# Up-projection as seven block products instead of eight, with weight-block sums made ahead

## The chip, the cores and the metric

One core of a Trainium2 chip runs the whole kernel. Its engines are TensorE (PE for the matrix products and PEld for their weight loads in the profile), VectorE (DVE), ScalarE (ACT), GpSimd (POOL) and SyncE (SP, which here only issues DMAs). The metric is the device time of one execution in microseconds (us), the median of several runs.

## The reference, cut to what matters

A decoder layer runs over 2048 prompt tokens and 64 sample tokens (8 sequences of 8). The first part (projections, sliding-window attention, the RWKV-7 recurrence) is not touched in what it computes. The second part is, per token:

```python
x = x + (g_a * (att @ w_pa) + g_b * (rw_out @ w_pb)) @ w_o
h = rmsnorm(x, norm2_g)
ug, uv = jnp.split(h @ w_up, 2, axis=-1)        # w_up: 1024 x 5632
c = conv_b + sum(conv_w[j] * ucat[:, j:j + T] for j in range(3))   # ucat: ug with 2 earlier rows
x = x + (jax.nn.gelu(c) * uv) @ w_down          # w_down: 2816 x 1024
y = rmsnorm(x, final_g)
```

## The kernel before, in words

The kernel has two phases. Phase 1 (`phase1`, `group1`) goes through the tokens in six groups, makes the combined input projection, attention and recurrence, and stores their outputs and the gates in DRAM (`outs_d`, `gates_d`). Its order on TensorE is written out: `mm` ties each product to the one before (`ordered`), and side work (attention, recurrence, the bias tables) runs as generators that yield a number of nanoseconds and are resumed when the planned time `now` has moved on by that much (`spawn`, `poll`, `drain`). The weights of the input projection come through the SP queue (`load_w`).

Phase 2 (`phase2`, `group2`) takes three groups of T = 704 tokens. All data is transposed: features on partitions, tokens along the free dimension. A product of fp32 quality is made of three products of rounded halves: both operands are split into a rounded part `hi` and a rest `lo`, and hi·hi, hi·lo and lo·hi are summed in PSUM. Weights are split as they arrive: `load_w` fetches up to [128, 8, 128] numbers, `split_w` lets ACT copy them into `whi` (L383) and `wsub` (L424) subtracts to get `wlo`; every second `wsub` goes to GpSimd (`pool_every` 2), the others to VectorE. Raw weights and their two halves share one pool tag of seven slots (`W_SLOTS`, `wtile`). Activations are split by ACT and VectorE in `split` (L1319 to L1323).

Each token group is two chunks of 352 columns; `gemm` (L471) goes over the k tiles, per k tile over the three passes, and per pass over both chunks, so a loaded weight tile serves two products of 352 columns. In a group come, in this order:

- eight output tiles of `w_ab` (attention and recurrence halves), gated on VectorE, added on GpSimd (L1386), split into `mix`;
- eight output tiles of `w_o`, added to x (L1399); VectorE and ACT split x times the norm weight into `h2` (L1323), and sum the squares (L1333);
- 22 pairs of feed-forward tiles in parts of 4, 6, 6 and 6: `up(f)` makes the `w_ug` tile, multiplies it by the row norm `rs` while taking it out of PSUM (L1427), runs the convolution (L1431, L1437) and the GELU (L1445 to L1448), and GpSimd multiplies by `rs` once more (L1449); `gate(f, s)` makes the `w_uv` tile, multiplies (L1456) and splits (L1323). The norm itself (`rstd_steps`) thus has the length of the first `up` product to finish in;
- after each part, eight output tiles of `w_down` over the 4 or 6 tiles of the part, added to x (L1478).

The final norm of a group (`final`) is spawned beside the next group's `w_ab`; for the last group it is the tail, made per chunk so that the first chunk's norm falls among the second chunk's last products.

Of the kernel before, what the change touches and what calls it, by code (L numbers as in the profile page):

```python
# [9 lines left out]
F32 = mybir.dt.float32  # L10
F32R = mybir.dt.float32r
# [68 lines left out]
Y_rwkv_post_2 = 1205  # L80
W_AT = (1, 5)
# [90 lines left out]
class Build:  # L172
# [315 lines left out]
    def phase1(self):  # L488
        nc, tc, cfg, A = self.nc, self.tc, self.cfg, self.A
        with ExitStack() as ctx:  # L490
# [4 lines left out]
                             at=AT_SLOTS, PTm=4, carry=2, sp=3, nrm=3, gm=2, gsq=1, XV=XV_SLOTS, Z=3, sm=8)  # L495
            self.pbufs = dict(acc=2, psA=2, ps=3, psY=1)
            self.cp1 = cp1
            self.rw = cfg.tmax + 9
            self.prev = dict(carry=None, vt=None, S=None)
# [91 lines left out]
    def group1(self, g, t0, n, samp, last):  # L591
# [72 lines left out]
        if g == 0:  # L664
            self.spawn(self.bias_tables())
        G.ready = 0
# [628 lines left out]
    def phase2(self):  # L1295
        nc, tc, cfg, A = self.nc, self.tc, self.cfg, self.A
        with ExitStack() as ctx:
# [3 lines left out]
            self.bufs = dict(A=16, B=16, x2=8, th=4, tm=2, ub=2, cc=2, ss=2, ssq=1, carry=2, nrm=3)  # L1301
            self.pbufs = dict(acc=8)
            for tag in ("B", "x2"):
                self.t(tag, [128, cfg.tmax2])
# [9 lines left out]
    def split(self, src, tag, T, scale=None):  # L1314
# [3 lines left out]
        if scale is None:  # L1318
            nc.scalar.copy(out=hi[:, :T], in_=src[:, :T])  # L1319
            nc.vector.tensor_tensor(out=lo[:, :T], in0=src[:, :T], in1=hi[:, :T].bitcast(F32), op=SUB)  # L1320
        else:
            nc.scalar.mul(out=hi[:, :T], in_=src[:, :T], mul=scale)  # L1322
            nc.vector.scalar_tensor_tensor(out=lo[:, :T], in0=src[:, :T], scalar=scale, in1=hi[:, :T].bitcast(F32), op0=MUL, op1=SUB)  # L1323
        return hi, lo

    def sumsq(self, ssq, x, m, T):
        nc = self.nc
        if m == 0:
            nc.scalar.activation(out=ssq[:, :T], in_=x[:, :T], func=AF.Square)
        else:  # L1330
            sq = self.t("ss", [128, self.cfg.tmax2])
            nc.scalar.activation(out=sq[:, :T], in_=x[:, :T], func=AF.Square)
            nc.vector.tensor_tensor(out=ssq[:, :T], in0=ssq[:, :T], in1=sq[:, :T], op=ADD)  # L1333

    def load_outs(self, c0, c1):
        self.outs, T = [], c1 - c0
        for k in range(8):
            o = self.t("th", [128, self.cfg.tmax2])
            self.last_load = self.nc.gpsimd.dma_start(out=o[:, :T], in_=self.outs_d[k][:, c0:c1]).ins.name
            self.outs.append(self.split(o, "A", T))  # L1340
# [18 lines left out]
    def group2(self, g, c0, c1):  # L1359
# [8 lines left out]
        chunks = [(i * w, (i + 1) * w if i < nchk - 1 else T) for i in range(nchk)]  # L1368
        if g == 0:
            self.load_outs(c0, c1)  # L1370
        outs = self.outs
        mix = []
        if g:
            done = self.spawn(self.later(L_SSQ, self.final(*self.done)))
        for m in range(8):
            hi, lo = self.weights("w_ab", m)
            self.nopool = False
            pa = self.gemm(hi, lo, outs[:4], 0, chunks, "acc")
            pb = self.gemm(hi, lo, outs[4:], 0, chunks, "acc", wk0=4)
# [7 lines left out]
            mix.append(self.split(ta, "B", T, 0.5))  # L1387

        if g:
            self.drain(done)  # L1390
        x2, h2 = [], []
        rs = self.t("ssq", [128, TM])
        for m in range(8):
            hi, lo = self.weights("w_o", m)
            ps = self.gemm(hi, lo, mix, 0, chunks, "acc")
            x = self.t("x2", [128, TM])
            nc.gpsimd.dma_start(out=x[:, :T], in_=A["x"][m][:, c0:c1])
            for (a, b), pp in zip(chunks, ps):
                nc.vector.tensor_tensor(out=x[:, a:b], in0=x[:, a:b], in1=pp[:, :b - a], op=ADD)  # L1399
            h2.append(self.split(x, "A", T, self.v("n2", m)))  # L1400
            self.sumsq(rs, x, m, T)
            x2.append(x)
        norm = self.spawn(self.later(L_SSQ, self.rstd_steps(rs, T, "acc")))
# [5 lines left out]
        while f < cfg.ff:  # L1409
            e = f + (cfg.ff - f - 1) % 6 + 1  # L1410
            parts.append(list(range(f, e)))
# [199 lines left out]
```

## Time and profile before

| | us |
|---|---|
| median of 3 runs (lowest, highest) | 3439.56 (3434.27, 3441.33) |
| profiled execution, run time | 3443.16 |
| profiled execution, span of the trace | 3441.4 |
| mean granted TensorE clock in it | 0.974 of 2.4 GHz |

Busy time of an engine is the union of its instructions' spans. The spans of products overlap their neighbours' (a 352-column product shows 0.32 us and the next one starts 0.16 us later), so a price per product is taken from the count of products in a stretch without idle time. The same holds, by some 0.08 us, for VectorE instructions that follow each other at once.

### The profile page before, as it was taken

To read this page: it belongs to the slowest core of one execution; us is meant where nothing else is said; L and a number is where in the kernel's file an instruction comes from. 1 tells how busy PE (TensorE), PEld (TensorE's weight loads), DVE (VectorE), ACT (ScalarE), POOL (GpSimd) and SP (SyncE) were. 2 spreads that over 40 slices of the span, in tenths; PEclk is the share of its full clock that TensorE was granted. 3 is DMA by queue.
4 is the path that set the end of the run, shared out by engine and by line. 5 is a ranking of instruction groups with operands and counts; after the bars stand their busy time and mean duration, and the time that the engine had idled before them with its cause. 6 is when DMAs were issued, how large, how long until landed. Compare 5 with 4: busy or idle time off the path is not lost.

```text
span 3441.4 us, 59346 instructions
## 1 busy us (share of the span) xinstructions
PE 3285.0 (95%) x23574; PEld 3134.0 (91%) x23574; DVE 1942.2 (56%) x3666; ACT 1161.1 (34%) x2370; POOL 1109.9 (32%) x1234
## 2 busy tenths in 40 slices
PE   7789889999999999989999999999999999999998
PEld 6778778888888888889999999999999999999998
DVE  6755746755655646655464455555464655564464
ACT  4443433433333433423232233232232323232232
POOL 4323423322223212152233332423243342343341
PEclk9898989999899999999999999999999999999999
DMA  6564656755655655562222223512222252222222
GB/s 201 187 202 165 218 171 212 250 182 192 217 172 192 217 196 190 169 206 76 68 66 70 68 67 123 176 59 76 69 68 74 91 179 73 62 69 73 68 68 73
DMA packets 197069, 460.74 MB, mean 134 GB/s; under 512 B 62719, under 2 KB 95111, under 8 KB 196791
## 3 DMA queue, kind: packets, MB, share of 16 engines
q1 hardware_dynamic: 169367, 396.86, 35.8%
q0 software_dynamic: 8704, 37.78, 3.4%
q10 hardware_dynamic: 18720, 22.31, 1.8%
q8 instruction: 185, 3.03, 0.4%
q14 instruction: 93, 0.76, 0.1%
HBM read 377.56 MB, written 79.31 MB: 133 GB/s over the span
## 4 chain that ended last, share of the span: by engine, by line
PE 78%; DVE 7%; DMA 5%; issue 3%; POOL 2%; ACT 2%; SPq 0%; DVEq 0%; POOLq 0%; ACTq 0%
PE acc L287 69%; PE ps L287 6%; PE psA L287 2%; DMA w<-w_in 2%; POOL wlo L424 1%; DVE LN L1034 1%; DVE TX L1032 1%; ACT whi L383 1%; DMA raw<-x 1%; DMA gates<-raw 1%; PE psY L287 1%; DVE wlo L424 1%; POOL th L1386 1%; DMA w<-w_ab 0%; DVE XV L1165 0%
## 5 line engine op out<-in xcount | busy, mean ns | idle before, releaser
L287 PE MATMUL acc<-A,whi 128*128 128x352 f32 x4992 | 1010.4, 324 | 3.7 <-DVE A L1320 3.1
L287 PE MATMUL acc<-h,whi 128*128 128x384 f32 (+2 forms) x3456 | 912.6, 343 | 24.7 <-ACT whi L383 12.9
L287 PEld LDWEIGHTS acc<-A,whi 128*128 128x128 f32 x4992 | 838.5, 188 | 5.5 <-DVE A L1320 4.0
L424 POOL TENSOR_TENSOR wlo<-w,whi 128x512 fp32r<-128x512 f32 (+2 forms) x347 | 480.9, 1386 | 1057.5 <-ACT whi L383 966.4
L383 ACT CAST whi<-w 128x512 fp32r<-128x512 f32 (+2 forms) x696 | 372.5, 581 | 1049.5 <-PE acc L287 551.8
L287 PEld LDWEIGHTS acc<-h,whi 128*128 128x128 f32 x3456 | 628.3, 196 | 56.8 <-ACT whi L383 15.4
L287 PE MATMUL acc<-h,wlo 128*128 128x384 f32 (+2 forms) x1728 | 587.0, 340 | 20.5 <-DVE wlo L424 16.5
L287 PE MATMUL acc<-A,wlo 128*128 128x352 f32 x2496 | 606.2, 324 | 0.0
L287 PE MATMUL acc<-B,whi 128*128 128x352 f32 x2880 | 583.7, 323 | 6.0 <-ACT B L1322 4.4
L287 PEld LDWEIGHTS acc<-B,whi 128*128 128x128 f32 x2880 | 482.8, 188 | 7.8 <-ACT B L1322 5.0
L287 PEld LDWEIGHTS acc<-A,wlo 128*128 128x128 f32 x2496 | 435.8, 188 | 0.1
L424 DVE TENSOR_TENSOR wlo<-w,whi 128x512 fp32r<-128x512 f32 (+2 forms) x349 | 295.2, 846 | 228.6 <-ACT whi L383 223.1
L287 PEld LDWEIGHTS acc<-h,wlo 128*128 128x128 f32 x1728 | 338.9, 196 | 38.9 <-DVE wlo L424 21.1
L287 PE MATMUL acc<-B,wlo 128*128 128x352 f32 x1440 | 350.6, 323 | 0.0
L287 PEld LDWEIGHTS acc<-B,wlo 128*128 128x128 f32 x1440 | 251.1, 188 | 0.0
L1478 DVE TENSOR_TENSOR x<-x,acc 128x352 f32<-128x352 f32 x188 | 89.3, 516 | 227.8 <-PE acc L287 227.8
L1449 POOL TENSOR_TENSOR ss<-ss,ssq 128x704 f32<-128x704 f32 x66 | 113.1, 1713 | 296.4 <-DVE ss L1448 274.6
L1437 DVE SCALAR_TENSOR_TENSOR cc<-ub,vt,cc 128x704 f32<-128x704 f32 (+1 forms) x132 | 147.6, 1118 | 35.2 <-ACT cc L1431 33.4
L1427 DVE TENSOR_TENSOR ub<-acc,ssq 128x352 f32<-128x352 f32 (+1 forms) x132 | 61.4, 507 | 124.5 <-PE acc L287 123.1
L1323 DVE SCALAR_TENSOR_TENSOR B<-ss,B 128x704 fp32r<-128x704 f32 x66 | 113.0, 1712 | 3.6 <-ACT B L1322 3.5
L1445 ACT ACTIVATE ss<-cc 128x704 f32<-128x704 f32 x66 | 52.3, 793 | 163.1 <-DVE cc L1437 110.6
L619 ACT COPY raw<-acc 128x384 f32<-128x384 f32 (+1 forms) x84 | 37.4, 445 | 182.9 <-PE acc L287 182.6
(302 smaller groups left out, 3596.1 us busy)
## 6 DMA issues: line engine op xcount, KB each, us to landing
whi<-w_in_hi SPq DMA_DIRECT2D x144, 512.0 KB, 4.6
wlo<-w_in_lo SPq DMA_DIRECT2D x144, 512.0 KB, 3.8
w<-w_in SPq DMA_DIRECT2D x72, 512.0 KB, 4.5
w<-w_ug SPq DMA_DIRECT2D x66, 512.0 KB, 3.5
w<-w_uv SPq DMA_DIRECT2D x66, 512.0 KB, 3.5
w<-w_down SPq DMA_DIRECT2D x72, 384.0 KB, 3.1
w_in_hi<-whi SPq DMA_DIRECT2D x36, 512.0 KB, 2.7
w_in_lo<-wlo SPq DMA_DIRECT2D x36, 512.0 KB, 5.1
```

The source lines that it names most:

```text
L287: self.pe(self.nc.tensor.matmul(out, lhsT, rhs, start=start, stop=stop), max(n * (1 if rhs.dtype == F32R else 4) / 2.4, 25))
L383: nc.scalar.copy(out=hi[:, a:b], in_=w[:, a:b])
L424: i = eng.tensor_tensor(**kw)
L619: nc.scalar.copy(out=raw[:, 1:1 + n], in_=acc[:, :n])
L1032: nc.vector.tensor_tensor(out=tv, in0=LN[:NL, j:j + 1, j + 1:32].broadcast_to([NL, j, w]), in1=LN[:NL, 0:j, j:j + 1].broadcast_to([NL, j, ...
L1034: nc.vector.tensor_tensor(out=LN[:NL, 0:j, j + 1:32], in0=LN[:NL, 0:j, j + 1:32], in1=tv, op=ADD)
L1323: nc.vector.scalar_tensor_tensor(out=lo[:, :T], in0=src[:, :T], scalar=scale, in1=hi[:, :T].bitcast(F32), op0=MUL, op1=SUB)
L1427: nc.vector.tensor_tensor(out=ub[:, 2 + a:2 + e], in0=pp[:, :e - a], in1=rs[:, a:e], op=MUL)
L1437: nc.vector.scalar_tensor_tensor(out=cc[:, :n], in0=ub[:, j:j + n], scalar=self.v(wn, f), in1=cc[:, :n], op0=MUL, op1=ADD)
L1445: nc.scalar.activation(out=s[:, :T], in_=cc[:, :T], func=AF.Square, scale=GELU_A)
L1449: nc.gpsimd.tensor_tensor(out=s[:, :T], in0=s[:, :T], in1=rs[:, :T], op=MUL)
L1478: nc.vector.tensor_tensor(out=x2[m][:, a:b], in0=x2[m][:, a:b], in1=pp[:, :b - a], op=ADD)
```

## The change

A pair of feed-forward tiles (256 rows of the result), the two halves of the 1024 input features and the two token chunks make a 2 x 2 by 2 x 2 block product. The change makes it from seven block products and sums of blocks (the variant of Strassen's method with 15 sums) instead of eight.

- Weight sums `s1` to `s4` of each block pair are made in phase 1 by a spawned generator: SP loads a quarter of four blocks, GpSimd makes four sums in place, SP stores them in DRAM (`sums_d`). 88 steps; they take one of the eight `sm` buffers and add two `ws` buffers.
- Operands: the row norm is now applied before the products, since blocks of different token chunks are subtracted. Every operand (`b11`, `b21`, `b22`, `t1` to `t4`, 4 k tiles each) is split by `split_half` (ACT copy, VectorE subtraction). To have the first chunk early, `w_o` goes over all eight tiles for chunk 0 and then for chunk 1, loading its weights twice; the norm of chunk 0 is made after two tiles of chunk 1. At the start of the feed-forward part the products 1 and 2, which need only chunk 0, are made for four runs (`fill`) while the norm and operands of chunk 1 come about. That stretch is ordered on TensorE; the rest of phase 2 is left to the planner of the tile framework (`self.ordered = False`).
- Products: each is 12 matmuls of 352 columns (4 k tiles, three passes) into one PSUM bank. Weights come two blocks at a time (`block_weights`), split per block. VectorE combines the seven results with four `put`s and three further additions per pair; ACT takes product 1 out of PSUM.
- `nopool` is set for all of phase 2, so all weight subtractions are on VectorE. The multiplication by `rs` on GpSimd (L1449) and the second factor in `split` (0.5, now applied when adding into x) are gone.

```diff
+Y_weight_sums_1 = 60000
+Y_weight_sums_2 = 6000
...
-            self.bufs = dict(A=16, B=16, x2=8, th=4, tm=2, ub=2, cc=2, ss=2, ssq=1, carry=2, nrm=3)
+            self.bufs = dict(A=56, B=12, x2=8, th=4, ub=2, cc=2, ss=4, u=4, u3=1, ug=1, ssq=1, carry=2, nrm=3)
+    def weight_sums(self):
+        yield Y_weight_sums_1
+        last = None
+        for i in range(self.cfg.ff // 2):
+            for x, wn in enumerate(("w_ug", "w_uv")):
+                for k in range(4):
+                    v = self.t("ws", [128, 4, 128])
+                    for j in range(2):
+                        nc.sync.dma_start(out=v[:, 2 * j:2 * j + 2], in_=self.A[wn][2 * i + j][:, k::4])
+                    if last:
+                        nc.sync.dma_start(out=last[0], in_=last[1])
+                    yield Y_weight_sums_2
+                    a11, a12, a21, a22 = (v[:, j] for j in range(4))
+                    for o, p, q, op in ((a22, a21, a22, ADD), (a21, a11, a21, SUB), (a11, a22, a11, SUB), (a12, a12, a11, SUB)):
+                        nc.gpsimd.tensor_tensor(out=o, in0=p, in1=q, op=op)
+                    last = self.sums_d[x][i][:, :, k], v
+                    yield Y_weight_sums_2
+    def block_weights(self, srcs):
+        w = self.wtile("w", F32)
+        for j, src in enumerate(srcs):
+            nc.sync.dma_start(out=w[:, j * 4:j * 4 + 4], in_=self.block_src(*src))
+        hi, lo = self.wtile("whi", F32R), self.wtile("wlo", F32R)
+        for j in range(len(srcs)):
+            a, b = j * 4, j * 4 + 4
+            nc.scalar.copy(out=hi[:, a:b], in_=w[:, a:b])
+            self.wsub(out=lo[:, a:b], in0=w[:, a:b], in1=hi[:, a:b].bitcast(F32), op=SUB)
+        return hi, lo
+    PRODUCTS = {1: ("b11", "a11"), 2: ("b21", "a12"), 3: ("b22", "s4"), 4: ("t4", "a22"), 5: ("t1", "s1"), 6: ("t2", "s2"), 7: ("t3", "s3")}
+    def product(self, R, p, wt, k0):
+        o = self.block_product(wt, k0, R.ops[self.PRODUCTS[p][0]])
+        def five():
+            R.put(1, 1, R.u3, R.p5)
+            nc.vector.tensor_tensor(out=R.u, in0=R.p5, in1=R.u, op=ADD)
+        ...
...
-            self.nopool = False
+            self.nopool = True
...
+        for c, (a, b) in enumerate(chunks):
+            for m in range(8):
+                hi, lo = self.weights("w_o", m)
+                if c == 1 and m == 7:
+                    self.ordered, self.last_pe = True, None
+                pp, = self.gemm2(hi, lo, mix, (c,))
...
+                if c == 1 and m == 1:
+                    for _ in norm(0):
+                        pass
+                    first_chunk()
...
+        def second_chunk(stage):
+            for j in range(4):
+                ...
+                if stage == 0:
+                    scaled(r, j, 1)
+                    nc.vector.tensor_tensor(out=p, in0=r, in1=p, op=SUB)
+                    ops["t1"][j] = self.split_half(p)
+                ...
...
+                fill = runs[:4]
+                for i, r in enumerate(fill):
+                    r.hold = i > 0
+                    self.run_products([(r, 1), (r, 2)])
+                    if i < 2:
+                        next(norm1, None)
+                        if i == 1:
+                            second_chunk(0)
+                for i in range(1, 5):
+                    second_chunk(i)
+                self.run_products([(runs[0], p) for p in (5, 6, 7, 4, 3)])
+                self.ordered = False
...
-                fin = self.spawn(self.later(L_TAIL, self.final(x2, ssq, c0, a, b, sqs)))
-            self.drain(fin)
+                self.spawn(self.later(L_TAIL, self.final(x2, ssq, c0, a, b, sqs)))
+            while self.procs:
+                self.drain(self.procs[0])
```

## Rows read from the trace of the kernel before

**Rows 1.** The page's parts 1 and 4: engines' busy time, and the chain by engine.
```profile
PE 3285.0 (95%) x23574; PEld 3134.0 (91%) x23574; DVE 1942.2 (56%) x3666; ACT 1161.1 (34%) x2370; POOL 1109.9 (32%) x1234
PE 78%; DVE 7%; DMA 5%; issue 3%; POOL 2%; ACT 2%; SPq 0%; DVEq 0%; POOLq 0%; ACTq 0%
```
**Rows 2.** Busy time by stretch: phase 1, phase 2, tail; columns named in the first line.
```profile
core 0: us, PE busy (x) PEld busy (x) DVE busy (x) ACT busy (x) POOL busy (x), PEclk, DMA share, GB/s
0.00:1488.00 1488.00, 1360.07 (x11636) 1212.92 (x11636) 910.25 (x2174) 561.12 (x1408) 439.17 (x605) 0.95 0.60 196
1488.00:3418.00 1930.00, 1915.69 (x11872) 1912.26 (x11873) 1019.67 (x1454) 595.83 (x954) 666.84 (x625) 1.00 0.28 86
3418.00:3441.40 23.40, 9.21 (x68) 8.80 (x67) 12.27 (x39) 4.13 (x8) 3.90 (x4) 0.68 0.35 124
```
**Rows 3.** Stretches of phase 2: up and gate products, then one of w_down.
```profile
1700.00:1750.00 50.00, 50.00 (x311) 50.00 (x311) 30.37 (x38) 16.73 (x25) 20.37 (x18) 1.00 0.25 75
...
3108.00:3157.00 49.00, 49.00 (x306) 49.00 (x305) 14.86 (x29) 10.10 (x18) 11.86 (x12) 1.00 0.26 78
```
**Rows 4.** Timeline of the last w_down products, one chunk alone (start us, us).
```profile
3412.40 0.48 PE L287 MATMUL acc<-B,whi 128*128 128x352 f32 x2
...
3412.88 0.48 PE L287 MATMUL acc<-B,whi 128*128 128x352 f32 x2
```
**Rows 5.** Timeline of VectorE in an up stretch (start us, us).
```profile
2915.66 0.69 DVE L424 TENSOR_TENSOR wlo<-w,whi 128x512 fp32r<-128x512 f32 x1 [1.53 <-ACT whi L383]
...
2932.34 0.89 DVE L1448 SCALAR_TENSOR_TENSOR ss<-ss,cc 128x704 f32<-128x704 f32 x1 [0.86 <-ACT ss L1447]
2933.15 0.95 DVE L1456 TENSOR_TENSOR ss<-ss,acc 128x352 f32<-128x352 f32 x2
2934.01 1.56 DVE L424 TENSOR_TENSOR wlo<-w,whi 128x512 fp32r<-128x512 f32 x1
2935.51 1.98 DVE L1323 SCALAR_TENSOR_TENSOR B<-ss,B 128x704 fp32r<-128x704 f32 x1
```
**Rows 6.** Timeline of GpSimd in the same stretch.
```profile
2933.32 1.72 POOL L1449 TENSOR_TENSOR ss<-ss,ssq 128x704 f32<-128x704 f32 x1 [4.58 <-DVE ss L1448]
```
**Rows 7.** VectorE by line and shape, 1700 to 3441 us (busy us, mean ns).
```profile
L424 DVE TENSOR_TENSOR wlo<-w,whi 128x512 fp32r<-128x512 f32 x156 | 159.1, 1020 | 100.3 <-ACT whi L383 100.0
L1437 DVE SCALAR_TENSOR_TENSOR cc<-ub,vt,cc 128x704 f32<-128x704 f32 x80 | 91.0, 1137 | 23.0 <-ACT cc L1431 21.6
```
**Rows 8.** Timeline of ACT in an up stretch.
```profile
2924.44 1.14 ACT L383 CAST whi<-w 128x512 fp32r<-128x512 f32 x2 [1.05 <-PE acc L287]
```
**Rows 9.** VectorE timeline around the norm before the third group's up products.
```profile
2909.42 0.88 DVE L1333 TENSOR_TENSOR ssq<-ssq,ss 128x704 f32<-128x704 f32 x1
...
2916.80 0.89 DVE L1427 TENSOR_TENSOR ub<-acc,ssq 128x352 f32<-128x352 f32 x2 [0.44 <-ACT ssq L465]
```
**Rows 10.** Stretches at a group's end, and where w_ab gives over to w_o.
```profile
2120.00:2130.00 10.00, 6.63 (x42) 6.34 (x40) 5.14 (x7) 3.66 (x6) 2.56 (x2) 0.97 0.19 55
2130.00:2140.00 10.00, 9.97 (x50) 9.75 (x51) 4.45 (x19) 2.04 (x4) 1.32 (x1) 0.69 0.17 52
...
2200.00:2210.00 10.00, 7.91 (x47) 7.62 (x48) 4.00 (x5) 3.46 (x5) 3.56 (x4) 1.00 0.57 177
```
**Rows 11.** GpSimd by line and shape in phase 1 (60 to 1150 us).
```profile
L424 POOL TENSOR_TENSOR wlo<-w,whi 128x512 fp32r<-128x512 f32 x63 | 90.5, 1437 | 168.4 <-ACT whi L383 132.0 <-PE ps L287 9.0 <-DMA outs<-xv 8.7
...
L1166 POOL TENSOR_TENSOR sp<-Z,PC 128x256 f32<-128x256 f32 x20 | 15.3, 764 | 76.8 <-DVE Z L1160 60.3 <-DVE gr L437 16.5
```
**Rows 12.** The page's DMA parts: queue (packets, MB, share), issues (KB, us to landing).
```profile
q1 hardware_dynamic: 169367, 396.86, 35.8%
...
w<-w_ug SPq DMA_DIRECT2D x66, 512.0 KB, 3.5
```
**Rows 13.** The end of the chain of waits, in order of time (start us, us).
```profile
3404.99 18.07 PE acc L287 x119
...
3426.01 3.21 DVE x L1356 x6
```

More of the change, by code (lines that the diff above doesn't have):

```diff
@@ L498, in phase1 @@
             self.rw = cfg.tmax + 9
+            self.sums_d = [[self.dram.tile([128, 4, 4, 128], F32, name=f"sums{x}{i}") for i in range(cfg.ff // 2)] for x in "gv"]
             self.prev = dict(carry=None, vt=None, S=None)
@@ L1339, in load_outs @@
             self.last_load = self.nc.gpsimd.dma_start(out=o[:, :T], in_=self.outs_d[k][:, c0:c1]).ins.name
-            self.outs.append(self.split(o, "A", T))
+            h = [self.split_half(o[:, c * w:c * w + w]) for c in range(2)]
+            self.outs.append(lambda c, h=h: h[c])
+    def weight_sums(self):
+        nc = self.nc
+        yield Y_weight_sums_1
[14 more added lines that the diff above has]
+                    yield Y_weight_sums_2
+        nc.sync.dma_start(out=last[0], in_=last[1])
@@ L1342, in later, with run_products @@
+    def run_products(self, seq):
+        for j in range(0, len(seq), 2):
+            two = seq[j:j + 2]
+            wt = self.block_weights([(R.x, R.i, self.PRODUCTS[p][1]) for R, p in two])
+            for k, (R, p) in enumerate(two):
+                self.product(R, p, wt, k * 4)
     def later(self, ns, gen):
@@ L1403, in group2 @@
-        norm = self.spawn(self.later(L_SSQ, self.rstd_steps(rs, T, "acc")))
+            if m < 6:
+                h = self.split(ta, "B", T)
+                mix.append(lambda c, h=h: [x[:, c * w:c * w + w] for x in h])
+            else:
+                h = [self.split_half(ta[:, a:b]) for a, b in chunks]
+                mix.append(lambda c, h=h: h[c])
+            if m:
+                next(done, None)
+        rs = self.t("ssq", [128, TM])
+        x2 = [self.t("x2", [128, TM]) for _ in range(8)]
@@ new lines, in gate, with put @@
+        def gate(f, ss, acts):
+            done, out = [0, 0], [None, None]
+            def put(row, c, s, ps):
+                a, b = chunks[c]
+                x = ss[row][:, a:b]
+                t = self.t("ug", [128, w])
+                nc.vector.tensor_tensor(out=t, in0=ps, in1=s, op=ADD)
+                nc.vector.tensor_tensor(out=x, in0=x, in1=t, op=MUL)
+                done[row] += 1
+                if done[row] == 2:
+                    out[row] = self.split(ss[row], "B", T)
+                    if None not in out:
+                        acts.extend(lambda c, h=h: [z[:, c * w:c * w + w] for z in h] for h in out)
+            return Run(1, f // 2, put)
```

237 lines of the change are left out of this document (166 added, 71 removed).

## The prediction

> **What bounds the kernel now.** I read the page's parts 1 and 4 first: TensorE is busy 95% of the span and makes up 78% of the chain of waits [rows 1]. Busy shares are averages, so the table of stretches comes next [rows 2]. It shows two different kernels. Phase 1 (0 to 1488 us) has TensorE at 1360 of 1488 us with a granted clock of 0.95: a chain through several engines. Phase 2 (1488 to 3418 us) has TensorE at 1916 of 1930 us at full clock, while VectorE has 1020 us, GpSimd 667 us and ACT 596 us of work. In a stretch of up and gate products TensorE has no idle time at all [rows 3]. So in phase 2 a product that goes is time that goes, as long as nothing else becomes late.
>
> **Price of a product.** 311 products in 50.00 us are 160.8 ns each [rows 3]. The change runs one chunk at a time into one PSUM bank (order hi, hi, lo), where before two chunks alternate; the nearest row is the end of the last `w_down`, which already does this: three products from 3412.40 to 3412.88, 160 ns each [rows 4]. So the new order costs nothing per product. By the Trainium skill ("TensorE: Matmul & The Clock Gate", section Back-to-back issue gap) an isolated warm product takes N/2.4 + 2.5 ns, which for 352 columns would be 149 ns, and the 792 products below would be worth 118 us; the row has 160.8 ns, and the measurement decides.
>
> **The change part by part.**
>
> *Products removed.* A pair of feed-forward tiles took 2 tiles x 8 k tiles x 3 passes x 2 chunks = 96 products, and takes 7 x 4 x 3 = 84. 11 pairs each for `w_ug` and `w_uv`, three groups: 12 x 22 x 3 = 792 products x 160.8 ns = **-127.3 us**. Products in `w_ab`, `w_o` and `w_down` stay as many.
>
> *VectorE in the up stretch.* This is the engine to watch: it gets all weight subtractions, 14 blocks per `w_ug`-`w_uv` double pair where before it had four of eight halves, and the additions. Prices from starts that follow each other at once: 0.81 us for a 704-column operation (2932.34 to 2933.15) and 0.43 us for one of 352 columns with PSUM (two in 0.86 us) [rows 5]. A subtraction of 128x512 shows 0.69 us when GpSimd is quiet; less the 0.08 us by which spans overlap, 0.61 us. Beside a GpSimd operation [rows 6] the same subtraction takes 1.50 us (2934.01 to 2935.51), and the mean over the phase is 1.02 us [rows 7]. Which price holds? GpSimd keeps only small copies in the up stretch after the change, so I take the quiet ones. Per double pair: 14 x 0.61 = 8.5; 7 `w_ug` and 11 `w_uv` operations of 352 columns, 18 x 0.43 = 7.7; convolution and GELU 8 x 0.81 and two splits x 0.81 = 8.1. Sum 24.3 us against 168 x 0.1608 = 27.0 us of TensorE: 90% where it was 61% (30.37 of 50) [rows 3]. A `w_ug` run alone has 13.8 us against 13.5, a `w_uv` run 10.6. So VectorE is not the bound on average, but it is in bursts.
>
> *What a burst costs.* The weights decide it. A set of two blocks serves 24 products, 3.9 us, where a set served 48, 7.7 us. Landing takes 3.5 us [rows 12], two casts 1.14 us [rows 8], the last subtraction 0.7 us: 5.3 us. Seven slots hold two sets and a raw tile, so a load starts some 7.7 us ahead: 2.4 us of cover. Nothing in the trace shows a queue this full. Lower bound zero (no idle at 61%); upper bound if the contended prices held: 14 x 1.02 + 7.7 + 4 x 1.14 + 6 x 0.9 = 32 us, 5 us over TensorE, x 33 = 165 us. I take 1.0 us per double pair, near the lower end, because the sum with quiet prices still leaves 10%: **+33 us**.
>
> *Row norm before the products.* Today the norm is hidden: from the last sum of squares (2909.42) to the first use of `rs` (2916.80) about 6.5 us pass in which the first up product runs [rows 9]. Now the second chunk's operands wait for it. They need 8 scalings, 16 subtractions and 20 splits, 44 x 0.43 = 18.9 us of VectorE. Cover: the eight products held in `fill`, 96 x 0.1608 = 15.4 us, and then the products 5, 6, 7, 4, 3, 1.9 us each. `t1` is ready at about 6.5 + 5.2 = 12, inside the cover. `b22`, the last, at 6.5 + 18.9 + five weight subtractions (3.0) = 28.4 us, wanted at 15.4 + 2.5 (norm products) + 4 x 1.93 = 25.6. So 3 us are missing at the least; with ACT's 20 casts and the order fixed by hand I take 5 per group, **+15 us** (0 to 36: none, or all that goes past the fill). The first chunk's 16 operations (6.9 us) lie in the second half of `w_o`, 31 us long with about 19 us of other VectorE work: no cost; without that cover 7 us per group. Loading `w_o` twice adds eight sets per group; also covered there.
>
> *Boundaries.* At a group's end TensorE is idle 3.4 of 10 us and the next 10 us have a clock of 0.69; where `w_ab` gives over to `w_o` it is idle 2.1 us [rows 10]. The first is a norm product standing in the written order before ready ones; that order is lifted there. The second waits for the last `mix` tile, now split by chunk. I take **-6 us** (-15 to +6).
>
> *Phase 1.* 352 sums of 128x128 on GpSimd: 0.76 us at 256 columns, 1.44 at 512 [rows 11], so about 0.43 at 128, an estimate: 150 us in 1056 us of planned time (88 steps of 12). They can only cost. DMA: 88 x 512 KB = 46 MB; 397 MB took 35.8% of the span, 3.1 us per MB [rows 12], so 143 us more on a share of 0.60 over 1488 us [rows 2], 0.70 afterwards. They are issued by SP, ahead of `w_in` loads, and the store waits for GpSimd; queued behind it are those loads, which run two tiles (some 8 us) ahead. DMA is 5% of the chain, 172 us [rows 1]; if its waits grow by a sixth, 29 us, and some 10 us for VectorE slowed beside GpSimd: upper end 40. Lower end -5, since the planner's order moves anyway. I take **+12 us**, nearer to the lower end as the loads run ahead.
>
> *Tail.* The first chunk's final norm no longer falls among the second chunk's products, which now are placed first. The chain's end has six scalings of that chunk (3.21 us) [rows 13] already after the last product; I add **+3 us** (0 to 8).
>
> *Nothing each:* GpSimd's L1449 and the factor in `split` go, off the path; ACT gains casts and copies but stays near 14 us in 27.
>
> Sum: -127.3 + 33 + 15 - 6 + 12 + 3 = -70 us. Profiled span 3441.4 - 70 = 3371; the run is 1.8 us longer, 3373; the median of the runs lay 3.6 us below that run: **3370 us**.
>
> **The rivals.**
>
> 1. *Everything hides.* VectorE's 10% suffices, and the norm fits: -127.3 + 3 (tail) + 6 (phase 1) - 6, about 3315 us; range 3305 to 3345. For it: no idle in any up stretch; against: that stretch had VectorE at 61%, not 90%.
>
> 2. *The weight pipeline becomes the bound (slower).* VectorE's instructions stand in one fixed queue. If subtractions for the next set stand behind results that wait for the current set, each of the 77 x 3 = 231 sets pays for it. The other terms sum to -103 us (without the 33), so from 103/231 = 0.45 us per set the kernel is slower. One subtraction (0.69 us) late in each set gives 159 us, 3496 us. For it: 2.4 us of cover against bursts of six to seven us of convolution and GELU. Against: those wait for ACT in between ([rows 5] shows 0.86 us before L1448), and a subtraction fits in such a gap.
>
> 3. *Phase 1 pays more.* At its upper end (+40 instead of +12) and 2 us per double pair in the up stretch: 3370 + 28 + 33 = 3431; range 3400 to 3440. For it: phase 1 is where waits are chained; against: loads run ahead.
>
> **How the numbers follow.** Forecast (3345 to 3400) 0.45; rival 1, 0.30; rival 3, 0.09; rival 2, 0.16. The range leaves out the lowest part of rival 1 and most of rival 2: 3312 to 3450. A measurement of this kernel can tell 0.2% (7 us). Faster by more: 0.45 + 0.30 + 0.07 of rival 3 + 0.01 of rival 2 = 0.83; same: 0.02 + 0.03 = 0.05; slower: 0.12.
>
> **What would show it.** Up stretches: idle time of TensorE under 4%, VectorE at about 90%, subtractions near 0.69 us rather than 1.02. If instead TensorE waits for `wlo` or `whi` in most sets, rival 2 holds. Between `w_o` and the first gate products: one gap of about 5 us per group, ended by VectorE's operands. Phase 1's end 7 to 17 us later than 1488. Products at 160 to 161 ns; any other number there, or a clock below 1.00 in the up stretch, would make the largest term wrong.

## The result and the profile after

The changed kernel takes 3526.01 us (median of 4 runs, 3523.05 to 3526.56), the kernel before 3437.17 (4 runs): a ratio of 1.0256, interval 1.0238 to 1.0274. It is slower by 89 us where 70 us of gain were forecast, and outside the range. The profiled execution has a span of 3523.7 us against 3441.4, so 82.3 us are to be explained.

The page's parts 1 and 4 of the kernel after, to be held against [rows 1]:

```profile
PE 3228.6 (92%) x22818; PEld 3032.6 (86%) x22818; DVE 2323.9 (66%) x4757; ACT 1342.9 (38%) x2796; POOL 790.0 (22%) x1245
PE 59%; DVE 21%; DMA 9%; issue 4%; ACT 3%; POOL 2%; SPq 1%; ACTq 0%; DVEq 0%; POOLq 0%
```

TensorE's busy time fell by 56 us only, though 792 products are gone, and VectorE's share of the chain rose from 7% to 21%. The table of stretches says where (columns as in [rows 2]; phase 1, phase 2, tail):

```profile
0.00:1527.00 1527.00, 1369.44 (x11622) 1213.22 (x11622) 938.69 (x2177) 558.88 (x1409) 608.41 (x954) 0.95 0.69 221
1527.00:3502.00 1975.00, 1851.56 (x11148) 1812.27 (x11149) 1372.53 (x2542) 780.30 (x1381) 177.45 (x288) 0.97 0.37 117
3502.00:3523.70 21.70, 7.55 (x50) 7.07 (x48) 12.68 (x38) 3.75 (x7) 4.19 (x4) 0.57 0.38 133
```

Phase 1 ends 39 us later, and phase 2, with 6% fewer products, is 45 us longer: TensorE now stands idle for 123 us of it (14 before), and its granted clock is 0.97 where it was 1.00. For exact cuts I took three events that both kernels have. The last `w_in` product of phase 1 moved from 1456.1 to 1498.0 (+41.9). From there to the last `w_down` product it is 2004.3 us instead of 1966.9 (+37.4). The tail is 21.4 instead of 18.3 (+3.1). The middle part holds the 127 us that were saved, so 37.4 + 127.3 = 165 us were lost in it.

Stretches of the kernel after, answering to [rows 3], tell what sort of loss that is. First two undisturbed ones, of up and gate products and of `w_down` products; then two in the second group's `w_o`, where the norm of its first chunk stands; then three at the end of the norm of its second chunk:

```profile
1772.00:1792.00 20.00, 20.00 (x127) 20.00 (x126) 13.71 (x24) 9.42 (x17) 2.53 (x3) 1.00 0.43 133
...
2000.00:2050.00 50.00, 50.00 (x315) 50.00 (x314) 20.98 (x41) 11.02 (x22) 0.00 (x0) 1.00 0.29 86
...
2280.00:2290.00 10.00, 7.24 (x51) 7.16 (x49) 5.62 (x16) 3.90 (x9) 0.00 (x0) 0.99 0.43 142
2290.00:2300.00 10.00, 9.08 (x42) 9.08 (x43) 7.95 (x21) 4.73 (x11) 0.00 (x0) 0.67 0.16 53
...
2330.00:2340.00 10.00, 5.13 (x33) 4.84 (x31) 9.05 (x21) 5.59 (x13) 0.00 (x0) 0.88 0.28 79
2340.00:2350.00 10.00, 3.57 (x12) 3.57 (x13) 10.00 (x23) 6.65 (x15) 0.55 (x1) 0.50 0.00 0
2350.00:2360.00 10.00, 9.91 (x58) 9.62 (x57) 5.97 (x12) 2.19 (x4) 1.80 (x4) 0.94 0.84 261
```

The price of a product has not changed, in the new block products (127 in 20.00 us, 157 ns) and in `w_down` (315 in 50.00 us, 159 ns). Such a count takes in one or two products at the edges; from start to start the median is 161 ns in the kernel after and 162 ns before. From 2340 to 2350 VectorE is busy without a break, nothing is loaded (0 GB/s), TensorE does 12 products instead of 63, and the clock, after TensorE stood idle for about half of the ten microseconds ahead, is at 0.50, the lower level (1.2 GHz). A smaller gap from 2280 on is followed by 0.67. What TensorE waits for in phase 2 (us in total, times, longest us):

```profile
PE acc L289 <- DVE wlo L426: 96.5, 65, 11.3
PE acc L289 <- ACT whi L1405: 11.8, 17, 1.1
PE acc L289 <- DVE nrm L454: 11.0, 3, 3.7
```

The first is the last step of preparing a weight set, the subtraction on VectorE; the third is the norm of the first chunk, once per group. The timeline of VectorE shows why the subtraction is late, in the first group (start us, us; L1524 scales, L1654 is an operand sum, L1333 a split, L426 the weight subtraction):

```profile
1666.15 1.08 DVE L1524 SCALAR_TENSOR_TENSOR th<-x,vt,ssq 128x352 f32<-128x352 f32 x2 [0.71 <-ACT ssq L467]
...
1682.64 0.53 DVE L1333 TENSOR_TENSOR A<-ss,A 128x352 fp32r<-128x352 f32 x1
1683.08 0.52 DVE L1654 TENSOR_TENSOR ss<-ss 128x352 f32<-128x352 f32 x1
1683.51 0.53 DVE L1333 TENSOR_TENSOR A<-ss,A 128x352 fp32r<-128x352 f32 x1
1683.95 0.69 DVE L426 TENSOR_TENSOR wlo<-w,whi 128x512 fp32r<-128x512 f32 x1
```

From 1666.15 to 1683.95 only scalings, operand sums and splits stand in VectorE's queue, 38 of the 44 operations of the second chunk; the next weight subtraction comes behind them. TensorE waits 11.0 us for it; at the same place of the second group it waits 11.3 us, the longest of the phase, and 10.9 us in the third.

Next, the up and gate products behind the norm and `w_down`, one row for each group:

```profile
1720.00:2182.00 462.00, 444.07 (x2671) 434.06 (x2670) 319.82 (x565) 184.08 (x318) 26.56 (x44) 0.98 0.35 109
...
2381.00:2841.00 460.00, 442.80 (x2669) 432.46 (x2668) 319.41 (x565) 183.75 (x318) 23.06 (x45) 0.99 0.35 109
...
3040.00:3502.00 462.00, 441.96 (x2670) 431.49 (x2671) 317.83 (x599) 180.42 (x319) 31.37 (x70) 0.99 0.33 101
```

2670 products at 160.8 ns are 429 us; the rows are 460 to 462 long. So 31 to 33 us are lost per group here, 96 in all. The hundred microseconds around the norm give more for their length:

```profile
1620.00:1720.00 100.00, 78.16 (x450) 76.12 (x449) 77.14 (x163) 47.03 (x87) 6.55 (x12) 0.88 0.32 102
...
2281.00:2381.00 100.00, 78.28 (x451) 76.25 (x451) 77.26 (x163) 46.97 (x87) 6.83 (x12) 0.88 0.33 102
```

450 products are 72.4 us, so 27.6 us are lost per group, 82 in all (the third group has 454 products). In the kernel before 100 us held 626 products and no idle time:

```profile
1600.00:1700.00 100.00, 100.00 (x626) 99.78 (x624) 54.42 (x83) 30.90 (x53) 27.85 (x27) 1.00 0.19 59
```

96 + 82 is 13 us more than the 165, since the kernel before had idle time and slower products of its own, at the ends of its groups [rows 10].

What VectorE does in an up stretch can be read between two `w_down`s, where three double pairs stand (504 products, 81.0 us at 160.8 ns). One of nine such stretches:

```profile
1909.20:1999.20 90.00, 84.75 (x505) 81.92 (x504) 72.35 (x122) 42.42 (x69) 7.05 (x12) 0.98 0.36 115
```

The nine take 90.4 us in the mean (88.6 to 92.2), with 74.1 us of VectorE (72.4 to 75.5). So VectorE's work is 24.7 us per double pair where 24.3 were forecast, and 3.1 us are lost per double pair where 1.0 was taken.

### The profile page after: what moved, and what is told of

Read it like the earlier page. It is cut to its first block, busy times and chain, and to the rows that moved or that the text cites. A ratio compares the mean times of both kernels' runs of the same rounds, so it can differ in the third digit from the quotient of the medians.

```text
span 3523.7 us, 60434 instructions
## 1 busy us (share of the span) xinstructions
PE 3228.6 (92%) x22818; PEld 3032.6 (86%) x22818; DVE 2323.9 (66%) x4757; ACT 1342.9 (38%) x2796; POOL 790.0 (22%) x1245
## 4 chain that ended last, share of the span: by engine, by line
PE 59%; DVE 21%; DMA 9%; issue 4%; ACT 3%; POOL 2%; SPq 1%; ACTq 0%; DVEq 0%; POOLq 0%
PE acc L289 52%; PE ps L289 4%; DVE wlo L426 3%; DVE cc L1587 3%; DMA w<-w_in 2%; DMA w<-sumsg 2%; PE psA L289 2%; DVE TX L1036 1%; DVE ss L1596 1%; DVE LN L1038 1%; POOL ws L1384 1%; DMA sumsv<-ws 1%; DVE ss L1598 1%; ACT whi L385 1%; DMA w<-w_o 1%
## 5 line engine op out<-in xcount | busy, mean ns | idle before, releaser
L289 PE MATMUL acc<-A,whi 128*128 128x352 f32 x4656 | 1108.6, 329 | 15.8 <-ACT whi L1405 11.8
L289 PEld LDWEIGHTS acc<-A,whi 128*128 128x128 f32 x4656 | 821.1, 192 | 27.6 <-ACT whi L1405 20.3
L289 PE MATMUL acc<-A,wlo 128*128 128x352 f32 x2328 | 736.0, 334 | 97.2 <-DVE wlo L426 96.5
L426 DVE TENSOR_TENSOR wlo<-w,whi 128x512 fp32r<-128x512 f32 (+2 forms) x870 | 571.2, 675 | 225.5 <-ACT whi L385 170.6
L385 ACT CAST whi<-w 128x512 fp32r<-128x512 f32 (+2 forms) x480 | 251.8, 564 | 542.8 <-DMA w<-w_down 187.8
L1405 ACT CAST whi<-w 128x512 fp32r<-128x512 f32 x462 | 271.0, 616 | 254.9 <-DMA w<-sumsg 82.2
L1585 POOL COPY carry<-ub 128x2 f32<-128x2 f32 x66 | 30.0, 455 | 1160.0 <-DVE ub L1610 1160.0
L1705 DVE SCALAR_TENSOR_TENSOR x<-acc,x 128x352 f32<-128x352 f32 x188 | 90.0, 520 | 205.6 <-PE acc L289 205.6
L1384 POOL TENSOR_TENSOR ws<-ws 128x128 f32<-128x128 f32 x352 | 191.1, 545 | 141.7 <-DMA ws<-w_uv 66.1
L426 POOL TENSOR_TENSOR wlo<-w,whi 128x512 fp32r<-128x512 f32 x72 | 101.8, 1415 | 104.2 <-ACT whi L385 83.9
L1323 ACT CAST B<-ss 128x704 fp32r<-128x704 f32 x66 | 51.6, 783 | 168.8 <-DVE ss L1627 168.8
L622 ACT COPY raw<-acc 128x384 f32<-128x384 f32 (+1 forms) x84 | 37.4, 445 | 183.0 <-PE acc L289 173.1
```

Of the source, the lines that this page charges most:

```text
L289: self.pe(self.nc.tensor.matmul(out, lhsT, rhs, start=start, stop=stop), max(n * (1 if rhs.dtype == F32R else 4) / 2.4, 25))
L385: nc.scalar.copy(out=hi[:, a:b], in_=w[:, a:b])
L426: i = eng.tensor_tensor(**kw)
L622: nc.scalar.copy(out=raw[:, 1:1 + n], in_=acc[:, :n])
L1384: nc.gpsimd.tensor_tensor(out=o, in0=p, in1=q, op=op)
L1405: nc.scalar.copy(out=hi[:, a:b], in_=w[:, a:b])
```

## The experiments

The theory after the result: VectorE's one fixed queue is the cause in phase 2, because weight subtractions stand in it behind bursts of other work; and in phase 1 the transfers of the weight sums, queued on SyncE, hold up the loads behind them. Each run of the kernel before beside these lay at 3439 to 3441 us (median).

### Phase 1: the weight sums alone

**The whole step added to the kernel before**, with nothing of phase 2:

```
+            self.spawn(self.weight_sums())
-   XV=XV_SLOTS, Z=3, sm=8)
+   XV=XV_SLOTS, Z=3, sm=7, ws=2)
```

> The kernel before with the generator of weight sums added to phase 1 (same loads, sums and stores, one softmax buffer fewer); phase 2 stays as before and does not use them. In the changed kernel the input-projection products run 41 us late from about 850 us on. If that lateness is the sums' own: run about 3437 + 41 = 3478 us, and the last 384-column projection product some 41 us later than before. If it comes from something else in phase 1 or its end: at most 10 us more, below 3450.

Measured: 3490.96 us, ratio 1.0155 (1.0116 to 1.0193); the last `w_in` product 48 us late. SyncE's waits from 60 to 860 us, first with the sums, then (after "...") without, in the kernel before:

```profile
SPq L1359 <- POOL ws L1363: 63.9, 25, 7.9
...
SPq L353 <- PE acc L287: 186.3, 49, 11.2
```

Before, SyncE's main wait was for TensorE to free a buffer: it was ahead. With the sums it stands 63.9 us in the store that waits for GpSimd. In the kernel after it is the same (63.4 us in 23 waits), and ACT's wait for the `w_in` tile behind it grew from 50.1 to 81.2 us.

**The transfers without GpSimd's sums:**

```
-   for o, p, q, op in (...): nc.gpsimd.tensor_tensor(out=o, in0=p, in1=q, op=op)
```

> As the sums alone, but without the four GpSimd operations per step: loads and stores only, the stored data is not summed. SyncE in the changed kernel waits 63 us for GpSimd's sums and 60 us for the stores between 60 and 860 us, with input-projection loads queued behind. Theory (SyncE's queue blocked behind the sums): without GpSimd a store waits only for its load, so at least half of the lateness goes: 10 to 20 us remain. Rival (46 MB more on the DMA engines): all but a few us remain, 33 to 41. Rival (GpSimd's time): 0 to 5 remain.

Measured: 3452.56 us, 1.0051 (1.0019 to 1.0082); the last `w_in` product 10 us late. Traffic and queue slots cost 10 us as long as nothing in them waits for an engine.

**GpSimd's sums without the transfers:**

```
-   nc.sync.dma_start(...)   # both loads and the store
+   nc.gpsimd.memset(v, 0.0)   # once
```

> As the sums alone, but without loads and stores: GpSimd makes the same 352 operations on a buffer of zeros. Theory (SyncE's queue): 0 to 8 us later than before, as nothing is added to SyncE. Rival (GpSimd's time, VectorE slowed beside it): 25 to 41 us.

Measured: 3574.21 us, 1.0397 (1.0367 to 1.0427). It doesn't answer the question: without loads to wait for, all 352 sums were placed between 3.7 and 239.5 us, ahead of GpSimd's own work, and the last `w_in` product was 135 us late.

**The same, with each sum tied behind the product last placed** (an order, not a wait), so that they are spread over phase 1:

```
+   z = nc.gpsimd.tensor_tensor(out=o, in0=p, in1=q, op=op)
+   self.tc.add_manual_dep(z.ins, self.last_pe, ORDER, reason="pace")
```

> The kernel before with the 352 GpSimd sums alone, on a buffer of zeros, without loads or stores, each placed behind the product that stood last in TensorE's order when the generator reached it; the run without this tie had them all in the first 240 us and says nothing on their cost when spread. With loads and stores alone phase 1 was 10 us late, with both 48. Theory (SyncE's queue blocked by stores that wait for GpSimd): 0 to 12 us late, 3437 to 3452. Rival (GpSimd's time and VectorE beside it): 25 to 40 us, 3462 to 3480.

Measured: 3459.03 us (8 runs), 1.0045 (1.0027 to 1.0064); 12 us late in the profiled execution. Transfers 10, sums 12, both together 48 by the last `w_in` product (13, 18 and 52 by the medians): 20 to 26 us appear only where both are there, and transfers can wait for sums. The comparison has a weakness. Here the sums run from 118 to 1373 us, with the whole step from 22 to 932 and in the kernel after from 22 to 927; the place of the sums in time differs too. Against that as the whole cause: from 60 to 860 us GpSimd is busy for 364 us here and for 395 with the whole step, and by the middle of the `w_in` products this run is 9 us late and that one 44.

**The transfers issued by GpSimd itself,** so that none waits in SyncE's queue:

```
-   nc.sync.dma_start(...)
+   nc.gpsimd.dma_start(...)
```

> As the sums alone, with the sums' loads and stores issued by GpSimd instead of SyncE; amount of data and GpSimd operations as there. Theory (SyncE's queue): the lateness falls to 5 to 20 us, since the input-projection loads have no wait for sums ahead of them. Rival (DMA engines' load): 33 to 41 us as in the sums alone. If GpSimd's own order becomes the trouble (its queue now also waits for loads): more than 41.

Measured: 3703.99 us, 1.0774 (1.0743 to 1.0806): a miss. The steps were all done by 642 us, GpSimd was busy for 493 us until then, and the last `w_in` product was 254 us late. The wait moved into GpSimd's queue, which has work on the chain too. It says nothing for or against SyncE's queue.

**Loads and stores tied behind the product last placed,** still on SyncE:

```
+   self.paced(nc.sync.dma_start(...))
+   def paced(self, i): self.tc.add_manual_dep(i.ins, self.last_pe, ORDER, reason="pace")
```

> The kernel before with the whole weight sums, as in the run with them alone (48 us late), but each load and each store placed behind the product that stood last in TensorE's order when the generator reached it, without any wait added. Loads and stores alone cost 10 us in phase 1, GpSimd's operations alone 11. Theory (the stores stand in SyncE's queue so early that they wait for GpSimd, with input-projection loads behind them): 12 to 25 us late, 3450 to 3465 us. Rival (the sum of data and GpSimd time does it, whatever the place): 40 to 50 us late, 3480 to 3490.

Measured: 3463.17 us (8 runs, 3452 to 3477; the profiled execution is the longest), 1.0055 (1.0037 to 1.0073). SyncE's longest waits are again those of a queue that is ahead:

```profile
SPq L355 <- PE acc L289: 125.4, 38, 10.3
SPq L371 <- ACT whi L385: 68.7, 16, 7.9
```

No wait for the sums is left among the main ones, and ACT's wait for `w_in` tiles is 47.9 us (75.8 with the sums unpaced). The cost is 22 us by the medians, where the whole step unpaced cost 52 and its two parts 13 and 18. So some 30 us can be had back by placing the transfers later. That it is their place in SyncE's queue fits SyncE's and ACT's waits; but the sums run later with them (112 to 1402 us), and no run moved the one without the other.

### Phase 2: who is late

**The sums of operands left out of the row norm's part:**

```
-   nc.vector.tensor_tensor(out=p, in0=r, in1=p, op=SUB); ops["t1"][j] = self.split_half(p)
+   ops["t1"][j] = ops["b11"][j]        # t2, t3 and t4 likewise
```

> The changed kernel without the 16 operand subtractions and 16 of the 20 splits of the second chunk: the operands t1 to t4 are replaced by b11, so the results of the up products are not the reference's; all products, weights and loads stay. From one 25 us stretch to the next TensorE loses some 30 us per group between the end of w_o and the second feed-forward run. Theory (operand sums hold up the subtractions in VectorE's queue): 14 us of VectorE less per group, and the clock's fall with the gap goes too: 15 to 25 us per group, 3450 to 3480 us in all. Rival (the norm itself, 6.5 us, makes the gap): at most 5 us per group, 3510 to 3526.

Measured: 3489.27 us, 1.0132 (1.0086 to 1.0177), 37 us less than the kernel after. Phase 1, which is the same code, was 13 us longer in this run's profiled execution, so I compare by products: from the first of `w_o` to the first of `w_down` there are 756 in both kernels, and they take 141.1, 139.8 and 141.6 us in the three groups where the kernel after takes 154.8, 153.8 and 155.8. That is 14 us per group, just below the 15 to 25 expected. At 160.8 ns these products are 121.6 us, so 33 us were lost there and 19 still are: scaling, the splits that are left, and the bursts behind would be the rest, which no run separates.

**Every second weight subtraction on GpSimd** in phase 2, then **every one:**

```
-   self.nopool = True
+   self.nopool = False                         # every second
+   self.nopool, self.pool_every = False, 1     # every one
```

> The changed kernel with every second weight subtraction of phase 2 back on GpSimd, as before the change. In the changed kernel TensorE waits 96 us in phase 2 for subtractions on VectorE, at moments when VectorE is busy without a break. Theory (VectorE's one queue makes the subtractions late): half of the subtractions find an idle GpSimd (1.3 us each instead of 0.6): phase 2 shrinks by 40 to 80 us, the run takes 3445 to 3485 us. Rival (the seven weight slots and the landing of loads): no change, 3520 to 3530. Rival (VectorE slowed beside GpSimd): slower than 3526.

> The changed kernel with all weight subtractions of phase 2 on GpSimd: 14 x 1.3 = 18 us of its time per 27 us of TensorE, VectorE freed of 8.5 of 24 us. Theory (VectorE's queue): at least as good as half of them, 3430 to 3485, unless GpSimd's 1.3 to 1.7 us, twice in a set of 3.9 us, become the bound; then TensorE waits for GpSimd instead and the run is above 3500.

Measured: 3643.33 us, 1.0586 (1.0549 to 1.0622), and 3610.6 us, 1.0484 (1.0442 to 1.0526). Both are far slower than the kernel after; relief for VectorE by GpSimd is a miss. VectorE by form, from 1650 us to the end: the subtraction in the kernel after and with half of them moved; after that the gate's multiplication (two SBUF operands) and the sum that reads PSUM, in the kernel after and with all moved:

```profile
L426 DVE TENSOR_TENSOR wlo<-w,whi 128x512 fp32r<-128x512 f32 x559 | 382.9, 704 | 84.7 <-ACT whi L1405 43.9 <-ACT whi L385 40.5
L426 DVE TENSOR_TENSOR wlo<-w,whi 128x512 fp32r<-128x512 f32 x281 | 283.2, 1008 | 100.2 <-ACT whi L1405 65.8 <-ACT whi L385 34.2
...
L1627 DVE TENSOR_TENSOR ss<-ss,ug 128x352 f32<-128x352 f32 x132 | 68.5, 519 | 0.4
L1627 DVE TENSOR_TENSOR ss<-ss,ug 128x352 f32<-128x352 f32 x132 | 128.8, 976 | 2.3
...
L1626 DVE TENSOR_TENSOR ug<-acc,u 128x352 f32<-128x352 f32 x132 | 69.0, 523 | 54.9 <-PE acc L289 54.0
L1626 DVE TENSOR_TENSOR ug<-acc,u 128x352 f32<-128x352 f32 x132 | 68.4, 519 | 9.0 <-PE acc L289 2.4
```

Beside a busy GpSimd, these two operations of VectorE with both operands in SBUF take 1.4 and 1.9 times as long (704 to 1008 ns, 519 to 976; others less, the split of a gate tile 885 to 990), and the one that reads PSUM takes what it took (523 and 519). The Trainium skill has this in "Advanced Engine Details and Errata", section GPSIMD Details: GpSimd shares a read and a write interface with VectorE and conflicts with VectorE's instructions that have two SBUF inputs. The trace agrees, with these numbers. With half of the subtractions moved TensorE's wait for VectorE grows from 96.5 to 138.7 us, and with all moved it waits for GpSimd, whose subtraction takes 1477 ns (half moved, then all):

```profile
PE acc L289 <- DVE wlo L426: 138.7, 80, 12.4
...
PE acc L289 <- POOL wlo L426: 66.9, 74, 3.6
```

The change's "all on the vector engine" is thus the best of the three.

**The subtractions let past the burst:** weight sets written ahead of the operand stages, the first chunk's norm in two steps, and the paced sums of above:

```
+   w56 = wset(5, 6); second_chunk(1); w74 = wset(7, 4); self.product(r0, 5, w56, 0)
+   second_chunk(2); self.product(r0, 6, w56, 4); w3 = wset(3); second_chunk(3)   # and so on
```

> The changed kernel with three mends: loads and stores of the sums placed as in the run before this one; the norm of chunk 0 in two steps, one w_o tile apart; and for the first run the weight sets of products 5 to 4 and 3 written ahead of the operand stages, so that their subtractions are not behind all 44 operand operations. Theory (what is late is late by its place in a queue): phase 1 regains 25 to 35 us, the norm of chunk 0 some 4 us per group, the first feed-forward run 8 to 12 us per group: 3526 - 30 - 12 - 30 = 3454, range 3435 to 3475. Rival (the amount of VectorE's work in that stretch decides): phase 1 alone gives, 3495 or above.

Measured: 3484.88 us, 1.0123 (1.0098 to 1.0148): 41 us less than the kernel after, about half of that in phase 1. It is a miss: some 20 us in phase 2 are less than the 42 expected. The three 11 us waits for a subtraction are gone, and so is that for the first chunk's norm, but many short ones took their place (phase 2 to 3480 us):

```profile
PE acc L289 <- DVE wlo L426: 65.4, 69, 2.8
PE acc L289 <- ACT whi L1408: 17.0, 20, 1.9
...
PE acc L289 <- DVE nrm L454: 0.4, 1, 0.4
```

The 756 products from `w_o` to `w_down` take 145.6, 147.2 and 149.7 us, 6 to 9 less than in the kernel after. This order doesn't cure it; from 1600 to 1720 us VectorE is busy for 99.7 of 120 us.

**VectorE's work beside the weights cut** (two convolution taps and two GELU multiplications per tile left out), weights untouched:

```
-   nc.vector.scalar_tensor_tensor(out=cc[:, :n], in0=ub[:, j:j + n], ...)
-   nc.vector.scalar_tensor_tensor(out=s[:, :T], in0=s[:, :T], scalar=1.0, in1=cc[:, :T], ...)   # twice
```

> The changed kernel without the two taps of the convolution over 704 or 640 columns and without both GELU multiplications on VectorE, 3.2 us per tile, so that the feed-forward values are not the reference's; ACT's steps, products, loads and operand sums stay. In the up stretches after the first runs TensorE loses some 60 to 70 us in all. Theory (VectorE full in bursts, at the end of a w_ug run): these losses all but vanish and so does a part of the loss in the first runs: 3526 - 60 to - 95, 3430 to 3466. Rival (weights late by their loads or the number of slots): at most 15 us, above 3510.

Measured: 3434.84 us, 0.9985 (0.9971 to 0.9998), 91 us less than the kernel after. In phase 2 TensorE's waits for the subtraction shrink to seven, and what is left is the gap at the norm:

```profile
PE acc L289 <- DVE wlo L426: 35.7, 7, 11.2
```

From 1700 to 2080 us 2288 products, 368 us, fill all but 12 of 380 us. Weight loads, casts, subtractions and slots are the same as in the kernel after. So the losses of the up stretches go when VectorE's other work goes.

**The rival: too few weight slots, loads too late.** One slot held through phase 2, six left of seven:

```
+   held = self.wtile("held", F32)     # written at the start and again at the end of phase 2
```

> The changed kernel with one of the seven weight slots held through all of phase 2. Theory (VectorE's queue): in every gap that a late subtraction ends VectorE is busy, so the cover of the slots is not what ran out first; but the cover shrinks from some 2.4 us per set, so 10 to 40 us more, 3536 to 3566. Rival (the seven slots are already the bound): each of the 231 sets pays a part of its 3.5 us of landing, over 100 us more, above 3626.

Measured: 3542.22 us, 1.0292 (1.0261 to 1.0324): 16 us more. TensorE's wait for subtractions is about the same (100.3 us, 96.5 in the kernel after). A ring that was the bound would have cost over 100 us more by the estimate put down ahead; it isn't. A deeper ring wasn't tried.

### Halves of the weights kept from the first group

The last theory says that fewer subtractions, not better placed ones, are wanted, and that the weights of the three groups are the same. So the halves made in the first group are stored by GpSimd's queue and loaded as halves in the second and third, without cast or subtraction, **for every second set, then for two of three,** on top of the mended version:

```
+   def keep(self, key, make, n):     # around block_weights and w_o
+       if key in self.kd: load whi and wlo from self.kd[key] by nc.sync
+       ...
+       if len(self.seen) % KEEP == 0:   # KEEP = 2; then: if len(self.seen) % KEEP, KEEP = 3
+           nc.gpsimd.dma_start(out=d, in_=t[:, :n].bitcast(F32))   # whi, wlo
```

> The mended kernel (3485 us), in which the first token group of phase 2 stores both halves of every second new weight set (up blocks and w_o) to DRAM, issued by the idle GpSimd, and the later uses load the halves instead of splitting the raw set again. Groups 2 and 3 thus have half of VectorE's weight subtractions (about 77 of 154 in their up products, 47 us per group less) and half of ACT's casts; group 1 keeps all of them and is the comparison within the run. Theory (VectorE's whole work in bursts decides, whichever operation it is): TensorE's losses in groups 2 and 3 fall from some 65 us each to 35 to 45, group 1 stays: 3425 to 3450 us. Rival (the convolution's chain at the end of a run is special, subtractions are not): 10 us at most, 3470 to 3490. Rival (loads: 1.5 times the bytes for weights): groups 2 and 3 lose more than before, above 3490.

> As the run before, with two of three sets stored and loaded in halves instead of one of two. Theory (VectorE's work): some 10 us less again, 3415 to 3440. Rival (loads, now some 220 GB/s in the up stretches where 115 were): TensorE waits for loads, 3440 or above.

Measured: 3450.65 us, 1.0029 (1.0013 to 1.0045), and 3429.70 us, 0.9964 (0.9951 to 0.9978). The second is 11 us faster than the kernel before, 0.4%: little, but the interval leaves out 1. Its three groups, in a profiled execution that was the longest of its ten runs:

```profile
1511.00:2194.00 683.00, 632.69 (x3707) 604.61 (x3706) 451.74 (x819) 257.52 (x456) 116.82 (x209) 0.97 0.61 209
2194.00:2808.00 614.00, 605.08 (x3735) 599.30 (x3734) 385.49 (x710) 190.19 (x330) 49.79 (x85) 0.99 0.54 184
2808.00:3416.00 608.00, 602.14 (x3735) 595.73 (x3734) 385.44 (x756) 190.28 (x334) 61.96 (x114) 1.00 0.52 177
```

The second and third group take 614 and 608 us where the kernel after takes 659 and 661, and the kernel before 647 and 654: 385 us of VectorE instead of 459. ACT's work fell with the casts too, from about 260 to 190 us, so this run doesn't tell the two apart; the run with the shortened convolution left the casts as they were. The groups are 33 and 46 us less than before, where the products removed are worth 42 per group; at 160.8 ns the 3735 products are 601 us. The first group, which makes and stores the halves, takes 683 instead of 661. And phase 1 still pays for the sums: its last `w_in` product is 30 us late.

## Why the prediction was wrong

Term by term, for the profiled execution (us):

| term | predicted | measured | from |
|---|---|---|---|
| products removed | -127.3 | -127 | 157 to 161 ns in undisturbed stretches |
| VectorE in the up stretch | +33 (0 to 165) | about +90 | 31 to 33 lost per group behind the norm, less what before lost |
| norm and operand sums, boundaries | +15 and -6 | about +75 to 82 | 27.6 lost per group around the norm |
| phase 1 | +12 (-5 to 40) | +42 | last `w_in` product |
| tail | +3 | +3 | last `w_down` product to the end |
| sum | -70 | +82 | span |

The two middle terms together are 165 by the cuts; how they share it is uncertain by some 10 us.

*What was right.* The price of a product [rows 4], and that the new order inside a block costs nothing. The choice of VectorE's quiet prices: the subtraction took 704 ns in the mean, where it was 1020 [rows 7], the convolution's step 946 where it was 1137. The sum made of them, 24.7 us per double pair against 24.3. The tail. And the sign of each cost.

*VectorE in the up stretch: 90% of load was taken for slack of 10%.* The load came out as forecast, 74.1 us of VectorE for 81.0 us of products. The term was mis-sized all the same, 33 instead of about 90, because I priced VectorE against TensorE as a sum over a double pair, and took a value near the lower end since "the sum with quiet prices still leaves 10%". But a set of weights has a due time every 3.9 us. In the 46 waits for a subtraction in phase 2 that are longer than 0.3 us, 92.5 us together, VectorE was at work all of the time: the subtraction stood behind convolution, GELU, sums and splits. Leaving out part of convolution and GELU, and nothing else, brought back 91 us. That was the mechanism of rival 2, which I gave 0.16. Its deciding point, 0.45 us per set, is passed only if the gap at the norm is counted in (165 us over 231 sets, 0.71); the 90 us of the up stretch alone are 0.39. So this term by itself would not have made the kernel slower: with the other terms as forecast it would have ended at about 3427 us. The norm and phase 1 did the rest. The argument against it, that a subtraction fits into the gaps where convolution waits for ACT, holds only if the written order puts it there.

*Idle time also cost clock.* Of the 165 us, 108 are more idle time of TensorE (24.8 before, 132.7 after, between the same two events). Nearly all of the rest is products that took longer, as at 2340 to 2350 us with a clock of 0.50. I priced gaps at their length; here half as much again came on top. The profile before had it: a gap at a group's end was followed by ten microseconds at 0.69 [rows 10].

*The norm and the operand sums.* I counted 3 missing microseconds from a schedule in which each stage's operands and weights are ready as soon as VectorE can make them, and took 5. The trace shows 27.6 per group. The failed step is that "five weight subtractions" were spread among the 44 operand operations in the sum, while in the queue 38 of the operations stand ahead of the next subtraction: 17.8 us (1666.15 to 1683.95) in which no set gets ready, and the loads stop too (0 GB/s in the second group). A second step was put at nothing without being priced: the norm of the first chunk, in the middle of `w_o`. TensorE waits 3.7 us for its steps in each group (the `nrm` line above), and the products behind run at a granted clock of 0.67 (42 in the ten microseconds from 2290); some 7 us are lost there. The first chunk's 16 operations, for which I had taken "no cost", come only after that wait. Without the operand sums 14 us per group came back; with the sets let past and the first norm in two steps, 6 to 9. For the rest, order against amount is argued and not shown. The boundaries did gain what was forecast or more: the 99 us from 2182 and from 2841 hold 0.6 and 1.8 us of idle time, where the second and third group before had 6.6 and 7.1 in all.

*Phase 1.* The term was mis-sized, 42 instead of 12, at what I had named as the upper end. I took the lower part because "the loads run ahead". The runs show that they stop doing so only with both: transfers alone 10, sums alone 12, both 48, and both placed later 22. What I left out of the count is the store that waits for GpSimd (63.4 us in 23 waits) with the `w_in` loads behind it in one queue: I named that wait, and gave it no price of its own. That the missing part is this wait is the likeliest reading, not shown alone, as the sums were moved together with the transfers. GpSimd's 128x128 sum took 545 ns, where 430 were estimated.

## What to carry to other kernels

When a change takes work from the bounding engine and gives an in-order engine 90% of load, price it by due times: how long a run of other instructions can stand ahead of the one that the bounding engine waits for, and what each miss costs in idle time and in clock after it. Look in each queue, DMA queues too, for a step that waits for a slow engine while urgent work stands behind it; in phase 1 placing such steps later gave back 30 of 52 us. And if such an engine is too full, moving its work to a neighbour may slow both; leaving out repeated work (weights split again for each group) was what paid.

## What the runs showed of the hardware

VectorE's slowdown beside GpSimd depends on where the operands are: 519 to 976 ns for two operands in SBUF, none (523, 519) with one of them in PSUM, 128x352 each. GpSimd's subtraction of 128x512 took 1477 ns when it did all of them, 2.1 times the 704 of VectorE in the kernel after. I had expected that GpSimd could be used as relief; at these prices it couldn't.
